# A fixed order on two engines for the main loop of two squared-ReLU MLPs

## The chip, the core and the metric

The kernel runs on one core of a Trainium2 chip. The metric is the device time of one execution in microseconds (us). Three runs of the kernel before took 2671.49 to 2674.87 us, median 2673.55 us.

The core's engines are named as in the profile: PE is TensorE (matmuls; PEld is its loading of weights), DVE is VectorE, ACT is ScalarE, POOL is GpSimd, SP is SyncE, which issues the DMAs. Each engine works through its own stream of instructions in order, and waits on semaphores for what others must finish first. Matmuls write to PSUM, which has 8 banks of 512 float32 a partition; here they are `bank[:, 0]` to `bank[:, 7]`.

## The reference

A trunk of two layers on x of 1024 positions by 1024 channels. Layer 0 mixes positions by gated linear attention and sparse attention, layer 1 by a spatial gating unit (SGU), and each is followed by an MLP:

```
def _squared_relu_mlp(x, w1, w2):          # w1: 1024 x 4096, w2: 4096 x 1024
    h = jax.nn.relu(x @ w1)
    return (h * h) @ w2
```

Each sub-layer f is applied as h = h + RMSNorm_post(f(RMSNorm_pre(h))). The change touches the MLPs alone.

## The kernel before

*Numbers in two halves.* Every float32 operand of a matmul is kept as a high and a low half: `split` (L149) makes the high half by a ScalarE copy (`acopy`, L137) and the low half by a VectorE subtraction (`sub`, L140). A product takes three matmuls of 512 columns: high x high, high x low, low x high (`PASS`, L36).

*Up-projection.* The 4096 hidden channels are cut into 32 chunks of 128. `fetch1` (L364) loads the columns of w1 for a chunk into a ring of two buffers (`raw`, 512 KB each) and multiplies them by the norm's gain on POOL (`gain`, L289). `put1` (L372) makes the halves in a ring of two (`w1r`; `ffa_w` in the profile). `f1(c, half)` (L350) computes one chunk for 512 positions: 24 matmuls into bank 0 or 1, then ReLU (L360) and square (L361) on ScalarE. Four such blocks belong to a pair of chunks: A11, A12 for positions 0 to 511 and A21, A22 for the rest.

*Down-projection.* For a pair of chunks it is a 2 x 2 product of blocks, (A11 A12; A21 A22) with (B11 B12; B21 B22) of w2, and is done with 7 products in place of 8. That takes 8 sums of blocks of 128 x 512: four of w2's blocks (`w_sums`, `w_prep`; the buffer `raw2` holds B, T1 is one more block) and four of the hidden blocks (`h_prep`). All 8 run on POOL (`minus` at L324, and the addition at L426). The seven operand pairs are split into `HS[0..6]` and `WS[0..6]` (`ffa_hTa`, `ffb_hTb` and `ffb_w` in the profile).

*Units.* `product(hh, i)` (L437) is one unit: the product i of 7 for one half hh of the 512 rows, 2 x 3 matmuls into a pair of banks, and two additions of the pair into `acc_of` (`ffb_acc`, L147). A pair of chunks has 14 units. `chain` gives bank pair, whether a new accumulation begins, and the target. The products that share a pair accumulate onto each other in PSUM, and each is read out in between. The pairs are banks 2/3, 6/7 and 4/5, the same for both halves.

*The loop.* It runs over 14 pairs p (`NS`) in each layer. An iteration emits the 14 units and, spread behind them, the 96 matmuls of the up-projection of the next pair (`ahead`, L451), then the preparation of its operands. The first iteration does 24 matmuls of the up-projection ahead of its first unit. The last four chunks are done plainly behind the loop (`out_proj`).

*What sets the order.* The kernel is written against a scheduler that keeps the data dependences and otherwise orders each engine's stream by its own model of when things will be ready. So the order in which the Python code emits units and preparation is a wish, and the streams differ from it.

Of the kernel before, what the change touches and what calls it, by code (L numbers as in the profile page):

```python
# [117 lines left out]
def tile_trunk(ctx, tc, x, norm_g, ffn_w1, ffn_w2, e_w_in, e_w_out, gla_w_gate, gla_b_gate,  # L118
# [27 lines left out]
    def add(o, a, b):  # L146
        dve.tensor_tensor(o, a, b, op=OP.add)  # L147
# [6 lines left out]
    def mm(o, lhsT, rhs, start, stop):  # L154
        pe.matmul(o, lhsT, rhs, start=start, stop=stop, skip_group_check=True)  # L155
# [167 lines left out]
    def minus(o, a, b):  # L323
        pool.tensor_tensor(o.f, a.f, b.f, op=OP.subtract)  # L324
# [4 lines left out]
    def ffn(l, hsrc, hdst, gi, nxt):  # L329
# [71 lines left out]
        def w_sums():  # L401
            minus(T1, B12, B11)
            minus(B12, B22, B12)

        def w_prep(i):

            split2((B11, B21, B11, T1, B12, B22, B21)[i], WS[i])
            if i == 0:
                minus(B11, B22, T1)
            if i == 1:  # L410
                minus(B21, B21, B11)

        def blocks(q):
            return [hf.get((2 * q + i, half)) for half in range(2) for i in range(2)]

        def h_prep(q, i):
            A11, A12, A21, A22 = blocks(q)
            if i == 0:
                split2(A11, HS[0])
                minus(A11, A11, A21)  # L420
            elif i == 1:
                split2(A12, HS[1])
                split2(A11, HS[4])
            elif i == 2:
                minus(A11, A22, A11)
                pool.tensor_tensor(A21.f, A21.f, A22.f, op=OP.add)  # L426
                split2(A11, HS[2])
                split2(A21, HS[3])
                minus(A12, A12, A11)
                split2(A12, HS[5])  # L430
                split2(A22, HS[6])


        chain = ((2, True, 0, 0), (6, True, 0, 0), (2, False, 0, 1), (4, True, 1, 1),
                 (2, False, 1, 1), (4, False, 0, 1), (2, False, 1, 0))

        def product(hh, i, first):  # L437
            b0, begin, ro, co = chain[i]
            for j in range(2):
                o = (2 * hh + j) * P  # L440
                for n, (a, b) in enumerate(PASS):
                    mm(bank[:, b0 + j, :], HS[i].r[:, a, o:o + P], WS[i].r[:, b],
                       begin and n == 0, n == 2)
            for j in range(2):
                o = acc_of[2 * hh + j + 4 * ro].f[:, co * 512:co * 512 + 512]
                if first and i in (0, 2, 3, 6):
                    acopy(o, bank[:, b0 + j, :])
                else:
                    add(o, o, bank[:, b0 + j, :])

        def ahead(q):  # L451
            a, b = 2 * q, 2 * q + 1
            yield from f1(a, 0)
            yield from f1(a, 1)
            put1(a + 2)
            yield from f1(b, 0)
            yield from f1(b, 1)
            put1(b + 2)

        fetch2(0)  # L460
        w_sums()
        for c in (0, 1):
            all_of(f1(c, 1))
            put1(c + 2)
            for i in ((0, 1, 2), (3, 4, 5, 6))[c]:
                w_prep(i)
        for i in (0, 1):
            h_prep(0, i)
        for p in range(NS):
            q, last = p + 1, p == NS - 1  # L470
            h_prep(p, 2)
            fetch2(q)
            for c in (2 * q + 2, 2 * q + 3):
                fetch1(c)
            if not last:
                w_sums()
            f = ahead(q)
            todo = 0
            while p == 0 and todo < 24:
                next(f)  # L480
                todo += 1
            for u in range(14):
                product(u // 7, u % 7, p == 0)
                n = 96 * (u + 1) // 14
                while todo < n:
                    next(f)
                    todo += 1
# [980 lines left out]
```

## Time and profile before

| | |
|---|---|
| median of three runs | 2673.55 us |
| the profiled execution | 2673.74 us |
| its span | 2671.9 us |
| PE busy | 2587.2 us, 97% |
| PE weight loads (PEld) | 2150.1 us, 80% |
| DVE busy | 1796.8 us, 67% |
| ACT busy | 1140.3 us, 43% |
| POOL busy | 743.5 us, 28% |
| mean granted clock of TensorE | 0.99 |

A busy TensorE is one that has a matmul in its pipeline, at whatever clock. So its busy share says little about how many matmuls a stretch holds; the count does. The first product of the loop of layer 0 starts 714.8 us into the span, that of layer 1 at 1989.5 us; each MLP with its loop takes about 640 us. [...]

### The profile page before, as it was taken

What the parts mean: (1) busy time and instruction counts of PE and PEld (TensorE: products, weight loads), DVE (VectorE), ACT (ScalarE), POOL (GpSimd) and SP (SyncE); (2) the same over time, 40 slices, a digit from 0 to 9 for tenths busy, and PEclk for the clock granted to TensorE, in tenths of its full rate; (3) what the DMA queues carried; (4) which work ended last, traced back from release to release, by engine and by line L of the source; (5) the groups of instructions that cost most, each with busy time, mean ns of one, the idle gap of its engine ahead of it and who ended that gap; (6) DMA issues with size and microseconds to landing.
All of it is one profiled execution on the core that took longest, in us unless ns stands there. A gap on an engine that the chain in (4) does not pass through costs nothing. (4 is left out here: it accounts for less than half of the span.)

```text
span 2671.9 us, 32503 instructions
## 1 busy us (share of the span) xinstructions
PE 2587.2 (97%) x12466; PEld 2150.1 (80%) x12466; DVE 1796.8 (67%) x2927; ACT 1140.3 (43%) x2127; POOL 743.5 (28%) x492
## 2 busy tenths in 40 slices
PE   8999999999999999999999999999999999999997
PEld 7888888888788887777877888888888888777786
DVE  5676578996757667776774248656675766777677
ACT  5556388885543333332354222242254333333233
POOL 2322133324433332333220011100142433333323
PEclk9999999999999999999999999999999999999999
DMA  4122211004311111111142101121241121111114
GB/s 131 52 61 75 60 44 37 17 13 153 139 48 54 49 48 48 48 53 35 63 140 81 47 24 48 40 95 40 78 135 42 46 63 45 51 48 48 40 40 142
DMA packets 150052, 168.31 MB, mean 63 GB/s; under 512 B 6549, under 2 KB 118409, under 8 KB 149897
## 3 DMA queue, kind: packets, MB, share of 16 engines
q1 hardware_dynamic: 149896, 166.24, 19.5%
q8 instruction: 98, 1.61, 0.2%
q14 instruction: 58, 0.47, 0.1%
HBM read 143.14 MB, written 23.07 MB: 62 GB/s over the span
## 5 line engine op out<-in xcount | busy, mean ns | idle before, releaser
L155 PE MATMUL bank<-base_x,ffa_w 128*128 128x512 f32 x3888 | 962.3, 392 | 2.7 <-DVE ffa_w L141 2.0
L155 PEld LDWEIGHTS bank<-base_x,ffa_w 128*128 128x128 f32 x3888 | 730.4, 189 | 159.1 <-ACT base_bnd L360 3.3
L147 DVE TENSOR_TENSOR ffb_acc<-ffb_acc,bank 128x512 f32<-128x512 f32 x784 | 520.6, 683 | 290.8 <-PE bank L155 282.1
L155 PE MATMUL bank<-ffb_w,ffb_hTb 128*128 128x512 f32 x1476 | 399.7, 395 | 17.5 <-DVE ffb_acc L147 15.3
L291 POOL TENSOR_TENSOR ffa_raw<-ffa_raw,base_cf 128x1024 f32<-128x1024 f32 x80 | 160.5, 2008 | 743.3 <-DMA ffa_raw<-in_ffn_w_dram 449.4
L155 PEld LDWEIGHTS bank<-ffb_w,ffb_hTb 128*128 128x128 f32 x1476 | 275.5, 189 | 90.7 <-DVE ffb_acc L147 29.0
L155 PE MATMUL bank<-ffb_w,ffa_hTa 128*128 128x512 f32 x1140 | 312.5, 398 | 25.1 <-DVE ffb_acc L147 21.7
L155 PEld LDWEIGHTS bank<-ffb_w,ffa_hTa 128*128 128x128 f32 x1140 | 216.5, 191 | 77.8 <-ACT ffa_hTa L138 12.2
L324 POOL TENSOR_TENSOR base_bnd<-base_bnd 128x512 f32<-128x512 f32 x84 | 125.9, 1499 | 299.7 <-DVE ffa_hTa L141 236.1
L155 PE MATMUL bank<-base_x,mv_w 128*128 128x512 f32 x768 | 185.8, 393 | 0.9 <-DVE nsq_qq L1166 0.9
L138 ACT ACTIVATE ffb_w<-ffb_raw 128x512 fp32r<-128x512 f32 x182 | 111.9, 622 | 171.4 <-PE bank L155 140.5
L141 DVE TENSOR_TENSOR ffb_w<-ffb_raw,ffb_w 128x512 fp32r<-128x512 f32 x182 | 159.7, 882 | 23.5 <-ACT ffb_w L138 23.4
L138 ACT ACTIVATE ffa_w<-ffa_raw 128x1024 fp32r<-128x1024 f32 x81 | 85.9, 1060 | 196.9 <-PE bank L155 185.0
L155 PEld LDWEIGHTS bank<-base_x,mv_w 128*128 128x128 f32 x768 | 140.7, 188 | 28.4 <-DVE nsq_qq L1166 1.1
L141 DVE TENSOR_TENSOR base_x<-bank,base_x 128x512 fp32r<-128x512 f32 x204 | 135.9, 683 | 30.7 <-ACT base_x L138 29.5
L141 DVE TENSOR_TENSOR ffa_w<-ffa_raw,ffa_w 128x1024 fp32r<-128x1024 f32 x81 | 105.0, 1297 | 64.6 <-ACT ffa_w L138 64.5
L138 ACT ACTIVATE base_x<-bank 128x512 fp32r<-128x512 f32 x204 | 117.6, 598 | 45.3 <-PE bank L237 27.1
L360 ACT ACTIVATE base_bnd<-bank 128x512 f32<-128x512 f32 x128 | 75.5, 590 | 128.5 <-PE bank L155 77.5
L138 ACT ACTIVATE ffb_hTb<-base_bnd 128x512 fp32r<-128x512 f32 x118 | 73.3, 627 | 121.1 <-PE bank L155 56.2
L141 DVE TENSOR_TENSOR ffb_hTb<-base_bnd,ffb_hTb 128x512 fp32r<-128x512 f32 x118 | 109.1, 929 | 20.6 <-ACT ffb_hTb L138 20.2
L138 ACT ACTIVATE ffa_hTa<-base_bnd 128x512 fp32r<-128x512 f32 (+1 forms) x93 | 59.7, 642 | 147.2 <-PE bank L155 83.6
L155 PE MATMUL bank<-nsa_kk,nsq_qq 128*128 128x512 f32 (+3 forms) x384 | 93.2, 353 | 4.1 <-ACT base_bnd L1285 2.1
(352 smaller groups left out, 3876.0 us busy)
## 6 DMA issues: line engine op xcount, KB each, us to landing
ffa_raw<-in_ffn_w_dram SPq DMA_DIRECT2D x64, 512.0 KB, 4.1
ffb_raw<-in_ffn_w_dram SPq DMA_DIRECT2D x30, 1024.0 KB, 4.8
hbuf<-base_bnd SPq DMA_DIRECT2D x24, 512.0 KB, 3.9
base_bnd<-hbuf SPq DMA_DIRECT2D x24, 512.0 KB, 3.5
ffa_raw<-in_o_w_in_dram SPq DMA_DIRECT2D x32, 256.0 KB, 2.9
ffa_raw<-in_o_w_in_dram SPq DMA_DIRECT2D x16, 512.0 KB, 4.0
gla_raw<-in_e_w_in_dram SPq DMA_DIRECT2D x30, 256.0 KB, 2.8
base_bnd<-in_x_dram SPq DMA_DIRECT2D x14, 512.0 KB, 3.4
```

Of the source, the lines that this page charges most:

```text
L138: act.activation(o, i, AF.Copy, **kw)
L141: dve.tensor_tensor(o, a, b, op=OP.subtract)
L147: dve.tensor_tensor(o, a, b, op=OP.add)
L155: pe.matmul(o, lhsT, rhs, start=start, stop=stop, skip_group_check=True)
L291: pool.tensor_tensor(raw, raw, gcol(gi)[:, k0:k0 + nk].unsqueeze(2).to_broadcast([P, nk, n]), op=OP.mult)
L324: pool.tensor_tensor(o.f, a.f, b.f, op=OP.subtract)
L360: act.activation(r.f, pb, AF.Relu)
```

## The change

Five things change in `ffn` and its helpers.

1. `keep` pins an instruction behind everything that was emitted before it on its engine (an edge of order, no wait). While `fixed[0]` is true, in the loop over the 14 units, every matmul, VectorE addition and VectorE subtraction is pinned. ScalarE, POOL and SyncE are not.
2. The 8 sums of an iteration move from POOL to VectorE (`minus` calls `sub`; A21 + A22 uses `add`).
3. The gain of w1 moves from one POOL operation of 128 x 1024 to eight ScalarE copies of 128 x 128 with a scale by partition.
4. A table of work by unit replaces the loose preparation. `before(p, u)` gives what is prepared with unit u: its sums and ScalarE copies are emitted ahead of the unit's matmuls, its VectorE subtractions behind the unit's two additions. `behind(p, u)` gives loads and sums behind the unit.
5. In the second half of the rows the bank pairs 2/3 and 6/7 are exchanged.

Over the kernel, VectorE gets 224 instructions more, ScalarE 512 more and POOL 288 fewer. The matmuls are the same in number and size.

```
+    def keep(ins):
+        if fixed[0]:
+            tc.keep_in_program_order(ins)
...
-        dve.tensor_tensor(o, a, b, op=OP.subtract)
+        keep(dve.tensor_tensor(o, a, b, op=OP.subtract))
...
-        pe.matmul(o, lhsT, rhs, start=start, stop=stop, skip_group_check=True)
+        keep(pe.matmul(o, lhsT, rhs, start=start, stop=stop, skip_group_check=True))
...
     def minus(o, a, b):
-        pool.tensor_tensor(o.f, a.f, b.f, op=OP.subtract)
+        sub(o.f, a.f, b.f)
...
-                gain(rw, gi, 0, KC, P)
+                for k in range(KC):
+                    acopy(rw[:, k], rw[:, k], scale=gcol(gi)[:, k:k + 1])
...
+        chain = ((0, True, 0, 0), (1, True, 0, 0), (0, False, 0, 1), (2, True, 1, 1),
+                 (0, False, 1, 1), (2, False, 0, 1), (0, False, 1, 0))
+        def unit(u, p):
+            hh, i = u // 7, u % 7
+            which, begin, ro, co = chain[i]
+            b0 = ((2, 6) if hh == 0 else (6, 2))[which] if which < 2 else 4
...
+        def before(p, u):
+            q, last = p + 1, p == NS - 1
+            work = []
+            if u < 4:
+                A11, A12, A21, A22 = blocks(p)
+                work += (([sums((sub, A11, A22, A11)), halves(A11, HS[2])]
+                          + ([] if p == 0 else [halves(B21, WS[6])])),
+                         [sums((add, A21, A21, A22)), halves(A21, HS[3])],
+                         [sums((sub, A12, A12, A11)), halves(A12, HS[5])],
+                         [halves(A22, HS[6])])[u]
+            if u == 4:
+                work += [halves1(2 * q + 1)]
+            if u == 7:
+                work += [halves1(2 * q + 2)]
...
+            elif u >= 8:
+                work += [halves((B11, B21, B11, T1, B12, B22)[u - 8], WS[u - 8])]
...
+        def behind(p, u):
+            q = p + 1
+            if u == 0:
+                fetch1(2 * q + 2)
+            if u == 1:
+                fetch2(q)
+            if u == 4:
+                fetch1(2 * q + 3)
...
+            if u == 5:
+                minus(T1, B12, B11)
...
+            fixed[0] = True
             for u in range(14):
-                product(u // 7, u % 7, p == 0)
...
+                work = before(p, u)
+                for w in work:
+                    next(w)
+                unit(u, p)
+                for w in work:
+                    all_of(w)
+                behind(p, u)
+                while done < 96 * (u + 1) // 14:
                     next(f)
-                    todo += 1
...
+                    done += 1
+            all_of(f)
+            fixed[0] = False
```

In the streams below, `ffa_w` with `base_x` are matmuls of the up-projection, `ffb_w` with `ffa_hTa` or `ffb_hTb` those of the units. A number behind a name is that of a buffer: `ffb_w_6217` to `ffb_w_6223` are WS[0] to WS[6] before, `ffb_w_6236` to `ffb_w_6242` after.

TensorE before, in an iteration past the middle of layer 0's loop, behind 8 matmuls of the up-projection and 3 of a unit:

```order
L155 MATMUL bank<-ffb_w_6219,ffa_hTa_6145 128x512 x3
L155 MATMUL bank<-ffb_w_6218,ffa_hTa_6144 128x512 x3
L155 MATMUL bank<-ffb_w_6219,ffa_hTa_6145 128x512 x3
L155 MATMUL bank<-ffb_w_6221,ffb_hTb_6224 128x512 x3
L155 MATMUL bank<-ffb_w_6218,ffa_hTa_6144 128x512 x3
L155 MATMUL bank<-ffb_w_6221,ffb_hTb_6224 128x512 x3
L155 MATMUL bank<-ffb_w_6223,ffb_hTb_6226 128x512 x6
L155 MATMUL bank<-ffb_w_6217,ffa_hTa_6144 128x512 x3
L155 MATMUL bank<-ffb_w_6220,ffa_hTa_6145 128x512 x4
L155 MATMUL bank<-ffb_w_6217,ffa_hTa_6144 128x512 x3
L155 MATMUL bank<-ffb_w_6220,ffa_hTa_6145 128x512 x2
L155 MATMUL bank<-base_x_72,ffa_w_6142 128x512 x20
```

Here 36 product matmuls, 39 with the 3 ahead of the first row, follow each other, of several units by threes, until the next 20 of the up-projection. TensorE after, from the first unit of an iteration:

```order
L162 MATMUL bank<-ffb_w_6236,ffa_hTa_6144 128x512 x6
L162 MATMUL bank<-base_x_71,ffa_w_6141 128x512 x6
L162 MATMUL bank<-ffb_w_6237,ffa_hTa_6144 128x512 x6
L162 MATMUL bank<-base_x_71,ffa_w_6141 128x512 x7
L162 MATMUL bank<-ffb_w_6238,ffa_hTa_6145 128x512 x6
L162 MATMUL bank<-base_x_71,ffa_w_6141 128x512 x7
L162 MATMUL bank<-ffb_w_6239,ffa_hTa_6145 128x512 x6
L162 MATMUL bank<-base_x_71,ffa_w_6141 128x512 x4
L162 MATMUL bank<-base_x_72,ffa_w_6141 128x512 x3
L162 MATMUL bank<-ffb_w_6240,ffb_hTb_6243 128x512 x6
```

Every unit stands as six, and 6 or 7 matmuls of the up-projection stand behind each; all iterations but the first have this order.

VectorE before, at the same place of the program as TensorE's rows:

```order
L147 TENSOR_TENSOR ffb_acc_6230<-ffb_acc_6230,bank 128x512
L147 TENSOR_TENSOR ffb_acc_6229<-ffb_acc_6229,bank 128x512
L147 TENSOR_TENSOR ffb_acc_6233<-ffb_acc_6233,bank 128x512
L147 TENSOR_TENSOR ffb_acc_6230<-ffb_acc_6230,bank 128x512
L147 TENSOR_TENSOR ffb_acc_6234<-ffb_acc_6234,bank 128x512
L141 TENSOR_TENSOR ffb_hTb_6224<-base_bnd,ffb_hTb_6224 128x512
L141 TENSOR_TENSOR ffb_w_6221<-ffb_raw_6216,ffb_w_6221 128x512
L147 TENSOR_TENSOR ffb_acc_6233<-ffb_acc_6233,bank 128x512
L141 TENSOR_TENSOR ffb_w_6219<-ffb_raw_6216,ffb_w_6219 128x512
L147 TENSOR_TENSOR ffb_acc_6234<-ffb_acc_6234,bank 128x512
L141 TENSOR_TENSOR ffb_hTb_6226<-base_bnd,ffb_hTb_6226 128x512
L141 TENSOR_TENSOR ffa_hTa_6145<-base_bnd,ffa_hTa_6145 128x512
```

The additions into `ffb_acc` stand in no order of units, with subtractions of halves between them. VectorE after, from the start of an iteration (the row `base_bnd<-base_bnd` with L148 is A22 - A11 or A12 - A11, that with L154 is A21 + A22):

```order
L148 TENSOR_TENSOR base_bnd<-base_bnd 128x512
L154 TENSOR_TENSOR ffb_acc_6246<-ffb_acc_6246,bank 128x512
L154 TENSOR_TENSOR ffb_acc_6247<-ffb_acc_6247,bank 128x512
L148 TENSOR_TENSOR ffa_hTa_6145<-base_bnd,ffa_hTa_6145 128x512
L148 TENSOR_TENSOR ffb_w_6242<-ffb_raw_6235,ffb_w_6242 128x512
L154 TENSOR_TENSOR base_bnd<-base_bnd 128x512
L154 TENSOR_TENSOR ffb_acc_6246<-ffb_acc_6246,bank 128x512
L154 TENSOR_TENSOR ffb_acc_6247<-ffb_acc_6247,bank 128x512
L148 TENSOR_TENSOR ffa_hTa_6145<-base_bnd,ffa_hTa_6145 128x512
L148 TENSOR_TENSOR base_bnd<-base_bnd 128x512
L154 TENSOR_TENSOR ffb_acc_6246<-ffb_acc_6246,bank 128x512
L154 TENSOR_TENSOR ffb_acc_6247<-ffb_acc_6247,bank 128x512
```

The sum for a later unit stands ahead of the two additions of a unit, and the subtraction of halves behind them.

ScalarE before, from a wide copy of w1 on in one iteration:

```order
L138 ACTIVATE ffa_w_6142<-ffa_raw 128x1024
L360 ACTIVATE base_bnd<-bank 128x512
L361 ACTIVATE base_bnd<-base_bnd 128x512
L138 ACTIVATE ffb_hTb_6224<-base_bnd 128x512
L138 ACTIVATE ffb_w_6221<-ffb_raw_6216 128x512
L138 ACTIVATE ffa_hTa_6145<-base_bnd 128x512
L138 ACTIVATE ffb_hTb_6226<-base_bnd 128x512
```

The ReLU and the square of a block stand behind the wide copy. ScalarE after, at the start of an iteration:

```order
L138 ACTIVATE ffa_w_6142<-ffa_raw 128x1024
L367 ACTIVATE base_bnd<-bank 128x512
L368 ACTIVATE base_bnd<-base_bnd 128x512
L138 ACTIVATE ffb_hTb_6245<-base_bnd 128x512
L138 ACTIVATE ffa_hTa_6145<-base_bnd 128x512 x2
L138 ACTIVATE ffb_hTb_6244<-base_bnd 128x512
L367 ACTIVATE base_bnd<-bank 128x512
```

Here it is the copy for the next iteration's second chunk that stands ahead of the ReLU and the square of A22, and the copies for HS[6], HS[2], HS[3] and HS[5] follow.

## Rows read from the trace of the kernel before

**Rows 1.** Share of the span and instructions of each engine, from the page.
```profile
PE 2587.2 (97%) x12466; PEld 2150.1 (80%) x12466; DVE 1796.8 (67%) x2927; ACT 1140.3 (43%) x2127; POOL 743.5 (28%) x492
```

**Rows 2.** By stretches: matmuls (x) behind PE, then PEld, DVE, ACT, POOL, granted clock.
```profile
715.00:1355.00 640.00, 617.52 (x2653) 499.44 (x2652) 439.80 (x614) 227.04 (x373) 208.39 (x136) 0.99 0.17 53
755.00:955.00 200.00, 200.00 (x884) 165.68 (x883) 132.73 (x186) 71.83 (x116) 71.44 (x45) 1.00 0.16 51
1035.00:1235.00 200.00, 182.92 (x755) 144.81 (x755) 146.80 (x197) 64.36 (x106) 72.96 (x47) 0.96 0.15 45
1989.50:2629.50 640.00, 619.84 (x2670) 502.09 (x2669) 442.98 (x613) 225.83 (x371) 208.45 (x136) 0.99 0.16 51
2029.50:2229.50 200.00, 200.00 (x884) 165.40 (x882) 136.64 (x187) 72.09 (x116) 71.97 (x46) 1.00 0.16 51
2309.50:2509.50 200.00, 185.30 (x771) 146.71 (x770) 148.59 (x200) 65.61 (x108) 72.97 (x47) 0.97 0.16 51
```

**Rows 3.** The same view at one hole, and right behind it.
```profile
1041.00:1046.00 5.00, 1.81 (x8) 1.21 (x7) 5.00 (x6) 1.89 (x3) 5.00 (x4) 0.96 0.00 0
1045.50:1052.50 7.00, 6.30 (x16) 4.36 (x16) 7.00 (x10) 2.25 (x5) 2.73 (x2) 0.51 0.19 48
```

**Rows 4.** TensorE's waits in layer 0's MLP: total us, times, longest us.
```profile
PE bank L155 <- DVE ffb_acc L147: 18.5, 20, 3.2
```

**Rows 5.** Timeline at that hole: start, us, engine, line, operation, idle before it.
```profile
...
1032.25 2.88 PE L155 MATMUL bank<-ffb_w,ffa_hTa 128*128 128x512 f32 x12
...
1037.27 3.07 DVE L147 TENSOR_TENSOR ffb_acc<-ffb_acc,bank 128x512 f32<-128x512 f32 x5
...
1039.69 1.89 POOL L291 TENSOR_TENSOR ffa_raw<-ffa_raw,base_cf 128x1024 f32<-128x1024 f32 x1
1040.26 1.88 DVE L141 TENSOR_TENSOR ffb_hTb<-base_bnd,ffb_hTb 128x512 fp32r<-128x512 f32 x1
...
1040.40 0.96 PE L155 MATMUL bank<-ffb_w,ffb_hTb 128*128 128x512 f32 x3 [0.24 <-DVE ffb_acc L147]
...
1041.55 1.71 POOL L426 TENSOR_TENSOR base_bnd<-base_bnd 128x512 f32<-128x512 f32 x1
1042.06 1.74 DVE L141 TENSOR_TENSOR ffb_w<-ffb_raw,ffb_w 128x512 fp32r<-128x512 f32 x1
...
1043.29 0.63 ACT L138 ACTIVATE ffa_hTa<-base_bnd 128x512 fp32r<-128x512 f32 x1 [1.50 <-POOL base_bnd L426]
1043.72 0.68 DVE L147 TENSOR_TENSOR ffb_acc<-ffb_acc,bank 128x512 f32<-128x512 f32 x1
...
1044.55 2.81 PE L155 MATMUL bank<-ffb_w,ffa_hTa 128*128 128x512 f32 x8 [3.19 <-DVE ffb_acc L147]
```

**Rows 6.** By tile: count, then shortest, median and longest in ns.
```profile
L141 DVE TENSOR_TENSOR ffb_w<-ffb_raw,ffb_w x182: 675/686/2406, 708.2 to 2622.7; 128x512 fp32r<-128x512 f32 x182
L324 POOL TENSOR_TENSOR ffb_raw<-ffb_raw x56: 1282/1297/2157, 708.9 to 2583.6; 128x512 f32<-128x512 f32 x56
...
L141 DVE TENSOR_TENSOR ffa_w<-ffa_raw,ffa_w x81: 1206/1226/2352, 642.1 to 2559.7; 128x1024 fp32r<-128x1024 f32 x81
```

**Rows 7.** ScalarE by form: count, busy us, mean ns, idle before.
```profile
L138 ACT ACTIVATE ffb_w<-ffb_raw 128x512 fp32r<-128x512 f32 x182 | 111.9, 622 | 171.4 <-PE bank L155 140.5 <-POOL ffb_raw L324 14.2 <-DVE ffb_acc L147 12.3
...
L138 ACT ACTIVATE ffa_w<-ffa_raw,base_cf 128x512 fp32r<-128x512 f32 x14 | 9.8, 722 | 5.2 <-PE bank L155 3.4 <-DMA ffa_raw<-in_o_w_in_dram 1.5
...
L193 ACT ACTIVATE base_cf<-base_cf 128x1 f32<-128x1 f32 x48 | 9.4, 198 | 9.9 <-DVE base_cf L204 8.0 <-DVE base_cf L267 1.7
```

**Rows 8.** Timeline of ScalarE at the end of a projection.
```profile
882.32 1.06 ACT L138 ACTIVATE ffa_w<-ffa_raw 128x1024 fp32r<-128x1024 f32 x1 [1.12 <-PE bank L155]
883.29 0.58 ACT L360 ACTIVATE base_bnd<-bank 128x512 f32<-128x512 f32 x1
883.90 0.64 ACT L361 ACTIVATE base_bnd<-base_bnd 128x512 f32<-128x512 f32 x1
```

**Rows 9.** Loads of w2: from issue to landing.
```profile
DMA to landing us min/median/max: 3.0/4.8/6.8
```

More of the change, by code (lines that the diff above doesn't have):

```diff
@@ L399, in ffn, with halves, sums @@
         B11, B12, B21, B22 = (raw2[:, i, j] for i in range(2) for j in range(2))
[L401 to L411, printed above, removed]
-        def blocks(q):
[L414 to L438, printed above, removed]
+        def blocks(q):
+            return [hf[2 * q + i, half] for half in range(2) for i in range(2)]
+        def halves(src, slot):
+            acopy(slot.r[:, 0], src.f)
+            yield
+            sub(slot.r[:, 1], src.f, slot.f[:, 0])
+        def sums(*ops):
+            for op, o, a, b in ops:
+                op(o.f, a.f, b.f)
+            yield
+        chain = ((0, True, 0, 0), (1, True, 0, 0), (0, False, 0, 1), (2, True, 1, 1),
[4 more added lines that the diff above has]
+            b0 = ((2, 6) if hh == 0 else (6, 2))[which] if which < 2 else 4
             for j in range(2):
@@ L451, in ahead @@
         def ahead(q):
[L452 to L458, printed above, removed]
-        fetch2(0)
[L461 to L468, printed above, removed]
-        for p in range(NS):
[L470 to L479, printed above, removed]
+            for c in (2 * q, 2 * q + 1):
+                for half in range(2):
+                    yield from f1(c, half)
@@ new lines, in before @@
+        def before(p, u):
[12 more added lines that the diff above has]
+                work += [halves1(2 * q + 2)]
+            if u >= 8 and last:
+                if u < 12:
+                    work += [halves((B11, B12, B21, B22)[u - 8], WS[u - 8])]
+            elif u >= 8:
+                work += [halves((B11, B21, B11, T1, B12, B22)[u - 8], WS[u - 8])]
+                if u >= 10:
+                    A11, A12, A21 = (hf.get((2 * q + i, half)) for i, half in
+                                     ((0, 0), (1, 0), (0, 1)))
+                    work += ([halves(A11, HS[0])], [], [halves(A12, HS[1])],
+                             [halves(A11, HS[4])])[u - 10]
+            return work
@@ new lines, in ffn @@
+        fetch2(0)
+        all_of(f1(0, 1))
+        all_of(halves1(2))
+        fetch1(3)
+        all_of(f1(1, 1))
+        minus(T1, B12, B11)
+        minus(B12, B22, B12)
+        split2(B11, WS[0])
+        minus(B11, B22, T1)
+        split2(hf[0, 0], HS[0])
+        minus(hf[0, 0], hf[0, 0], hf[0, 1])
+        split2(B21, WS[1])
+        minus(B21, B21, B11)
+        split2(hf[1, 0], HS[1])
+        for i, b in ((2, B11), (3, T1), (4, B12)):
+            split2(b, WS[i])
+        split2(hf[0, 0], HS[4])
@@ L480, in ffn @@
+        for i, b in ((5, B22), (6, B21)):
+            split2(b, WS[i])
+        for p in range(NS):
+            f, done = ahead(p + 1), 0
+            while p == 0 and done < 24:
                 next(f)
[L481 removed]
+                done += 1
+            fixed[0] = True
             for u in range(14):
[L483 to L487 removed]
```

37 lines of the change are left out of this document (22 added, 15 removed).

## The prediction

> **What bounds the kernel now.** I read the shares of the engines first [rows 1]: TensorE is busy for 97% of the span and VectorE for 67%, so only time in which TensorE issues below its full rate can be won. The second view is the table by stretches, taken over the two MLPs [rows 2]. What to see there is the count of matmuls, not the busy time, since TensorE is also "busy" while it runs at half clock. A quiet stretch of 200 us in either MLP holds 884 matmuls of 512 columns, one every 0.2262 us. In 640 us that would be 2829. The MLP of layer 0 has 2653 and that of layer 1 has 2670, so 176 and 159 matmuls are missing, or 39.8 and 36.0 us: 75.8 us in all. They are not spread evenly. One stretch of 200 us in each loop (755 and 771 matmuls) lacks 129 and 113 of them, and its granted clock is 0.96 and 0.97, which by itself is 8 and 6 us. The rest, some 62 us, is waiting.
>
> The third view is the list of waits, which puts TensorE's waiting down to VectorE's additions into `ffb_acc`: 18.5 us in 20 waits, and the same again in the second loop [rows 4]. The fourth is the timeline of one such place [rows 5], and it says why the additions are late. The scheduler has put 12 product matmuls side by side and has no up-projection left to go between the next ones. Then the operands are missing. POOL does a gain of 1.89 us ahead of the sum that the next operand needs, and while POOL works two subtractions on VectorE take 1.88 and 1.74 us. The addition that would free the bank stands behind both, so TensorE stops for 3.19 us. At 1041 to 1046 us TensorE is busy for 1.81 of 5 us, and right behind that it gets 0.51 of its clock for about 7 us [rows 3]. [...] So a hole is paid for twice.
>
> **The change, part by part.**
>
> *Order on TensorE and VectorE.* An iteration is 14 units of 6 product matmuls plus 96 of the up-projection: 180 matmuls, 180 x 0.2262 = 40.7 us, 2.9 us a unit. After, 6 or 7 up-projection matmuls stand behind every unit, so between two uses of one bank pair lie another unit and two such groups: 6 + 7 + 7 matmuls, 4.5 us, in which the two additions must be done. Two additions take 1.3 us when nothing stands ahead of them. Exchanging banks 2/3 and 6/7 in the second half keeps that true where one half of the chain meets the other; with the old numbers the second half would begin on the pair that the first had just finished, with 7 matmuls (1.6 us) between.
>
> *Load on VectorE.* Per iteration: 28 additions, 14 subtractions of halves and now 8 sums, 50 instructions of 128x512, and two of 128x1024. VectorE has no such sum in the trace of before. The nearest row is the subtraction for `ffb_w`: median 0.686 us, longest 2.406 [rows 6]. The long ones are those that meet POOL: in the timeline 1.88, 1.74, and the POOL ops beside them 1.71 to 1.89 [rows 5]. After, POOL has nothing to do in the loops, so I take the median. Lower bound: five additions in a row take 3.07 us, which is 0.60 apart. So 50 x 0.60 to 0.69 and 2 x 1.23 [rows 6] is 32.5 to 37.0 us of 40.7. It fits, and VectorE's growth lies beside TensorE's work; if it did not fit, the whole loop would run at VectorE's pace (a rival below).
>
> *Load on ScalarE.* The gain goes from one POOL op to eight ScalarE ops of 128 columns, 16 an iteration. Such an op is not in the trace. Bounds: 0.198 us for one column and 0.722 us for 512 columns with a scale by column [rows 7]; a straight line between gives 0.33, so 5.3 us an iteration (3.2 to 11.6). With 14 halves at 0.62 [rows 7], two wide copies at 1.06 and four pairs of ReLU and square at 0.58 + 0.64 [rows 8], ScalarE has 21 us of 40.7, at worst 27. It hides behind TensorE. [...]
>
> *The start of an iteration* is the tightest place. VectorE's first instruction there is A22 - A11, and A22 is the last up-projection of the iteration before. On ScalarE the wide copy for `ffa_w` stands ahead of its ReLU and square; the three take 2.22 us from start to end [rows 8]. Queued on VectorE behind that subtraction are both additions of unit 0 and the lower half of the operand of unit 2: 2.2 + 0.7 + 1.3 + 0.7 = 4.9 us after the end of that projection. TensorE needs this half after unit 0, 6 matmuls, unit 1, 7 matmuls and the first two of unit 2, 27 x 0.2262 = 6.1 us, less 0.2 us for the pipeline of the last matmul. Unit 3 follows 2.9 us later, with about 3.1 us of VectorE work before it. So there is 0.8 to 1.0 us to spare, and I cost it at nothing.
>
> *A new wait.* T1 = B12 - B11 stands behind the additions of unit 5 on VectorE, and waits for the 1 MB of w2; behind it stand the additions of unit 6. The buffer comes free when unit 0's halves are done (5.5 us into the iteration), landing takes 3.0 to 6.8 us [rows 9], so the data is there at 12.3 us at the latest, and the subtraction's turn comes at 17.5. Nothing is lost. The DMAs keep their number and sizes.
>
> *What stays or is added.* Ahead of the loop five sums come to VectorE, and the first up-projection of chunk 2 is now pinned ahead of unit 0; it needs the chunk's halves, a ScalarE copy of 1.06 and a subtraction of 1.23 us, of which the last 14 matmuls of the chunk before it cover 3.2 us, if VectorE is free. Units 0 to 3 of the first iteration follow each other without up-projection between. I bound this by 0 and 5 us a layer and take 2.5, so 5 us. Outside the MLPs the order is as before.
>
> **Sum.** The profiled execution took 2673.7 us, its span 2671.9 us; the median of the runs is 2673.55, so it stands for them. 2673.7 - 75.8 + 5 = **2603 us**, a gain of 2.6%.
>
> **Rivals.**
>
> *A short stall in every iteration* (chance 0.13). If the start of an iteration is 1 us later than I count (0.8 to 1.0 to spare), every one of the 28 loses about 1 us at units 2 and 3: 2603 + 28 = 2631. For it: VectorE's fixed order lets nothing pass a late A22. Against: the later units have 2 us and more, so a delay does not add up.
>
> *The clock falls by itself* (0.06). If short waits remain, and the granted clock of the worst stretches (0.96) [rows 2] becomes that of both loops, 28 x 40.7 x 0.04 = 46 us come back: 2649. Against: the quiet stretches use the same three bank pairs at 1.00, and the low clock in rows 3 follows a hole. [...]
>
> *Given back outside* (0.08). The gain comes, but the prologues, or the ScalarE gains inside the stages before, cost 25 us a layer more than the 2.5 I take: about 2650. Nothing in the profile asks for it.
>
> *VectorE becomes the bound, and the kernel slower* (0.04). Place: the 24 SBUF subtractions and sums of an iteration. If the long ones were not POOL's doing, an op would cost c, and an iteration 28 x 0.60 + 22c + 2 x 1.8c = 16.8 + 25.6c us. It passes 40.7 us at c = 0.93, eats the whole gain (2.5 us in each of 28) at c = 1.03, and at c = 1.16, a usual long one in the timeline, it is 46.5 us: 28 x 5.8 = 162 us, 2765. Against: the median is 0.686.
>
> *It does nothing* (0.02): the holes move to other places of the same size, 2673.
>
> **How the numbers follow.** The forecast has 0.67, with 2594 to 2614 as its own range (0 to 5 us a layer of added cost, and a few matmuls that I may have put down to the loops wrongly). The range that holds 8 in 10 takes in the first rival and reaches toward the next two: 2594 to 2640. About 0.2%, 5 us, is what a measurement of this kernel can tell from no change. Faster: 0.67 + 0.13 + 0.06 + 0.08 = 0.94; same 0.02; slower 0.04.
>
> **What would show it.** Right: in the MLPs the stretches hold 177 matmuls per 40 us throughout and the granted clock is 1.00 there; VectorE's 128x512 subtractions have a mean near 0.69 us in place of 0.88; POOL is nearly empty in the loops; TensorE's waits for `ffb_acc` are gone. Wrong: VectorE busy without a gap while TensorE waits for it, a wait in every iteration at units 2 and 3, or a clock below 1.00 with no hole ahead of it.

## The result and the profile after

The changed kernel takes 2597.4 us (median of four runs, 2595.65 to 2597.74) against 2672.87 us before: ratio 0.9716, interval 0.9699 to 0.9733. It is 75.5 us faster; the forecast was 2603, 70 us faster.

The profiled execution took 2597.74 us. Its shares of the span, from the page:

```profile
PE 2555.6 (98%) x12466; PEld 2148.0 (83%) x12466; DVE 1856.6 (72%) x3151; ACT 1301.7 (50%) x2639; POOL 295.2 (11%) x204
```

The table by stretches, with the columns of [rows 2]; the first three rows have the windows of layer 0's rows there, the last is layer 1's loop:

```profile
715.00:1355.00 640.00, 640.00 (x2837) 530.04 (x2836) 505.68 (x802) 323.27 (x647) 12.94 (x6) 1.00 0.19 62
755.00:955.00 200.00, 200.00 (x884) 165.62 (x883) 167.02 (x254) 98.77 (x200) 0.00 (x0) 1.00 0.17 53
1035.00:1235.00 200.00, 200.00 (x884) 165.59 (x883) 167.93 (x256) 94.90 (x190) 0.00 (x0) 1.00 0.17 53
1960.00:2570.00 610.00, 610.00 (x2692) 504.99 (x2691) 480.07 (x740) 292.89 (x586) 8.76 (x4) 1.00 0.17 55
```

TensorE is never idle here, its clock is 1.00, and the stretch that held 755 matmuls holds 884. In the same 640 us there are 2837 matmuls in place of 2653. TensorE's waits over the whole span (total us, times, longest):

```profile
PE bank L184 <- DMA base_bnd<-in_gla_norm_dram: 4.8, 1, 4.8
PE bank L244 <- DVE base_bnd L261: 4.3, 1, 4.3
PE bank L162 <- ACT base_bnd L1330: 3.0, 5, 1.9
PE bank L244 <- DVE in_y L238: 2.2, 1, 2.2
PE bank L162 <- DVE ffa_w L148: 2.1, 1, 2.1
```

The additions into `ffb_acc`, which led this list before [rows 4], do not appear. By tile (count, shortest/median/longest ns, as in [rows 6]), VectorE's subtraction for `ffb_w` and the new gain pieces on ScalarE:

```profile
L138 ACT ACTIVATE ffa_raw<-ffa_raw,base_cf x512: 384/387/407, 638.9 to 2501.7; 128x128 f32<-128x128 f32 x171
...
L148 DVE TENSOR_TENSOR ffb_w<-ffb_raw,ffb_w x182: 683/686/693, 709.3 to 2521.4; 128x512 fp32r<-128x512 f32 x182
```

The subtraction's longest is 693 ns, where before it was 2406. A timeline of ScalarE (start, us, then the row) has one gain:

```profile
867.48 2.46 ACT L138 ACTIVATE ffa_raw<-ffa_raw,base_cf 128x128 f32<-128x128 f32 x8 [2.70 <-DMA ffa_raw<-in_ffn_w_dram]
```

Eight pieces take 2.46 us. Each is 0.39 long by itself, but they overlap: their starts are 0.29 apart (0.31 for the first two).

The start of an iteration in the timeline, on TensorE, then ScalarE and VectorE. Unit 0 starts at 880.27, unit 1 at 882.99, unit 2 at 885.94:

```profile
880.27 1.52 PE L162 MATMUL bank<-ffb_w,ffa_hTa 128*128 128x512 f32 x6
881.63 1.52 PE L162 MATMUL bank<-base_x,ffa_w 128*128 128x512 f32 x6
882.99 1.52 PE L162 MATMUL bank<-ffb_w,ffa_hTa 128*128 128x512 f32 x6
884.35 1.75 PE L162 MATMUL bank<-base_x,ffa_w 128*128 128x512 f32 x7
885.94 1.52 PE L162 MATMUL bank<-ffb_w,ffa_hTa 128*128 128x512 f32 x6
...
880.24 1.06 ACT L138 ACTIVATE ffa_w<-ffa_raw 128x1024 fp32r<-128x1024 f32 x1 [0.73 <-PE bank L162]
...
882.48 0.69 DVE L148 TENSOR_TENSOR base_bnd<-base_bnd 128x512 f32<-128x512 f32 x1 [1.71 <-ACT base_bnd L368]
883.09 1.28 DVE L154 TENSOR_TENSOR ffb_acc<-ffb_acc,bank 128x512 f32<-128x512 f32 x2
884.29 0.68 DVE L148 TENSOR_TENSOR ffa_hTa<-base_bnd,ffa_hTa 128x512 fp32r<-128x512 f32 x1
```

The wide copy waits for the end of A22's projection and starts at 880.24. The half (the row `ffa_hTa<-base_bnd,ffa_hTa`) that unit 2 needs is done at 884.97, and the third matmul of unit 2 wants it at 885.94 + 2 x 0.2262 = 886.39. So 1.4 us are to spare.

### The profile page after: what moved, and what is told of

Its sections match the earlier page's. It is cut to its first block, busy times and chain, and to the rows that moved or that the text cites. A ratio compares the mean times of both kernels' runs of the same rounds, so it can differ in the third digit from the quotient of the medians.

```text
span 2596.0 us, 33054 instructions
## 1 busy us (share of the span) xinstructions
PE 2555.6 (98%) x12466; PEld 2148.0 (83%) x12466; DVE 1856.6 (72%) x3151; ACT 1301.7 (50%) x2639; POOL 295.2 (11%) x204
## 4 chain that ended last, share of the span: by engine, by line
PE 87%; DVE 5%; ACT 3%; issue 2%; DMA 1%; POOL 1%; SPq 0%; DVEq 0%; POOLq 0%; ACTq 0%
PE bank L162 85%; PE bank L1346 1%; DVE base_x L148 1%; PE bank L244 1%; DVE base_cf L1329 1%; DVE mv_P L1339 1%; ACT base_x L138 1%; POOL mv_P L260 0%; ACT base_bnd L1330 0%; DMA base_bnd<-in_e_w_out_dram 0%; DMA base_bnd<-in_x_dram 0%; DVE sgu_v L683 0%; ACT mv_P L1330 0%; ACT base_bnd L210 0%; DMA base_bnd<-rbuf 0%
## 5 line engine op out<-in xcount | busy, mean ns | idle before, releaser
L154 DVE TENSOR_TENSOR ffb_acc<-ffb_acc,bank 128x512 f32<-128x512 f32 x784 | 524.5, 685 | 137.9 <-PE bank L162 134.7
L162 PE MATMUL bank<-ffb_w,ffb_hTb 128*128 128x512 f32 x1476 | 374.8, 389 | 0.0
L138 ACT ACTIVATE ffa_raw<-ffa_raw,base_cf 128x128 f32<-128x128 f32 x512 | 156.9, 389 | 267.6 <-DMA ffa_raw<-in_ffn_w_dram 267.6
L162 PE MATMUL bank<-ffb_w,ffa_hTa 128*128 128x512 f32 x1140 | 288.1, 389 | 0.0
L260 POOL TENSOR_TENSOR ffb_acc<-ffb_acc,base_bnd 128x1024 f32<-128x1024 f32 x15 | 36.0, 2400 | 1287.8 <-ACT base_bnd L210 1283.9
L148 DVE TENSOR_TENSOR base_x<-bank,base_x 128x512 fp32r<-128x512 f32 x204 | 136.0, 683 | 33.5 <-ACT base_x L138 32.4
L148 DVE TENSOR_TENSOR ffb_w<-ffb_raw,ffb_w 128x512 fp32r<-128x512 f32 x182 | 124.6, 686 | 8.5 <-ACT ffb_w L138 4.4
L148 DVE TENSOR_TENSOR ffa_w<-ffa_raw,ffa_w 128x1024 fp32r<-128x1024 f32 x81 | 99.8, 1234 | 41.7 <-ACT ffa_w L138 41.5
L1329 DVE TENSOR_REDUCE base_cf<-bank 128x1 f32<-128x640 f32 (+7 forms) x128 | 88.5, 698 | 12.1 <-PE bank L162 11.5
L162 PE MATMUL bank<-base_x,nsa_V 128*128 128x512 f32 x264 | 94.4, 431 | 2.6 <-DVE base_x L148 1.3
```

Of the source, the lines that this page charges most:

```text
L138: act.activation(o, i, AF.Copy, **kw)
L148: keep(dve.tensor_tensor(o, a, b, op=OP.subtract))
L154: keep(dve.tensor_tensor(o, a, b, op=OP.add))
L162: keep(pe.matmul(o, lhsT, rhs, start=start, stop=stop, skip_group_check=True))
L260: pool.tensor_tensor(acc, acc, gpost.f, op=OP.mult)
L1329: dve.reduce_max(out=nm, in_=sc[:, 0:W], axis=AX, negate=True)
```

## The experiments

| kernel | order | banks | sums and gain | us | ratio to before, interval |
|---|---|---|---|---|---|
| before | scheduler | old | POOL | 2672.9 | |
| changed | pinned | exchanged | moved | 2597.4 | 0.9716 (0.9699 to 0.9733) |
| order_only | pinned | exchanged | POOL | 2613.1 | 0.9770 (0.9755 to 0.9784) |
| moves_only | scheduler | old | moved | 2669.9 | 0.9983 (0.9973 to 0.9992) |
| old_banks | pinned | old | moved | 2602.4 | 0.9728 (0.9714 to 0.9743) |
| free | scheduler | exchanged | moved | 2597.5 | 0.9713 (0.9699 to 0.9728) |
| banks_only | scheduler | exchanged | POOL | 2599.5 | 0.9726 (0.9712 to 0.9741) |
| moves_banks | scheduler | exchanged | moved | 2597.4 | 0.9720 (0.9705 to 0.9734) |
| free_old_banks | scheduler | old | moved | 2669.2 | 0.9984 (0.9974 to 0.9994) |
| one_pin | one matmul pinned | old | POOL | 2642.4 | 0.9886 (0.9869 to 0.9902) |
| pool_sums | pinned | exchanged | only sums on POOL | 2608.6 | 0.9768 (0.9752 to 0.9785) |
| pool_gain | pinned | exchanged | only gain on POOL | 2600.9 | 0.9735 (0.9720 to 0.9749) |
| dve_14 | as changed, 14 subtractions more | | | 2727.9 | 1.0208 (1.0193 to 1.0223) |
| dve_7 | as changed, 7 subtractions more | | | 2599.9 | 0.9729 (0.9715 to 0.9744) |

My theory was the prediction's: the fixed order earns the time, with POOL emptied so that VectorE's additions are not late; the banks are a side condition.

### Parts of the change alone

**order_only**: the changed kernel with sums and gain given back to POOL.

```
-        sub(o.f, a.f, b.f)
+        pool.tensor_tensor(o.f, a.f, b.f, op=OP.subtract)
...
-                for k in range(KC):
-                    acopy(rw[:, k], rw[:, k], scale=gcol(gi)[:, k:k + 1])
+                gain(rw, gi, 0, KC, P)
```

> The changed kernel with its fixed order, but the 8 sums of an iteration and the gain of w1 back on POOL as before. Theory A (order): the holes came from an order that ran out of up-projection matmuls between units, so the fixed order alone removes them. VectorE's subtractions stay long beside POOL (mean near 0.88 us), 28 x 0.60 + 14 x 0.88 + 2 x 1.3 = 31.7 us of 40.7, which fits; the sum A22 - A11 takes 1.3 to 1.7 us on POOL where VectorE took 0.7, which uses up most of the 0.8 to 1.0 us to spare: 2597 to 2612 us. Theory B (contention): the holes came from subtractions that POOL makes long, and in an order that lets nothing pass they cost at least 1 us in each of 28 iterations: 2630 us or more.

2613.1 us, 1 us above the range of theory A and far below theory B. It keeps most of the gain, and past the first iterations its loops have no wait of TensorE. Nearly all that it lacks lies ahead of the loops and in their first iterations: from each MLP's first up-projection matmul to the end of the loop's first iteration TensorE loses 12.4 us more than in the changed kernel, of the 13.5 us by which the two profiled executions differ.

**moves_only**: the kernel before with sums and gain moved, the scheduler's order and the old banks.

```
-        pool.tensor_tensor(o.f, a.f, b.f, op=OP.subtract)
+        sub(o.f, a.f, b.f)
...
-                pool.tensor_tensor(A21.f, A21.f, A22.f, op=OP.add)
+                add(A21.f, A21.f, A22.f)
...
-                gain(rw, gi, 0, KC, P)
+                for k in range(KC):
+                    acopy(rw[:, k], rw[:, k], scale=gcol(gi)[:, k:k + 1])
```

> The kernel before in its free order, with only the sums moved to VectorE and the gain to ScalarE. Theory A (order): the scheduler still bunches units, holes and half clock stay for the most part, 2640 to 2680 us. Theory B (contention): without POOL beside it VectorE keeps up, and most of the 75 us is gone, 2600 to 2620 us.

2669.9 us: the move earns 0.17%. A stretch of its trace, then its first wait over the whole span and that of the kernel before:

```profile
1035.00:1235.00 200.00, 188.88 (x806) 150.66 (x805) 153.58 (x239) 88.77 (x184) 0.00 (x0) 0.99 0.15 46
```

```profile
PE bank L155 <- DVE ffb_acc L147: 33.8, 45, 1.9
...
PE bank L155 <- DVE ffb_acc L147: 37.0, 40, 3.2
```

POOL does nothing in this stretch, and still 78 of 884 matmuls are missing and TensorE waits for the additions. POOL was not what made the holes. The longest wait is shorter (1.9 us against 3.2), there are more of them, and the total is nearly the same.

**old_banks**: the changed kernel without the exchange.

```
-            b0 = ((2, 6) if hh == 0 else (6, 2))[which] if which < 2 else 4
+            b0 = (2, 6, 4)[which]
```

> The changed kernel without the exchange of bank pairs in the second half: units 6 and 7, and 13 and the next 0, use banks 2/3 with 7 up-projection matmuls (1.6 us) between. If the exchange matters: the additions need 0.2 + 0.7 us for the first bank and 0.6 more for the second, so VectorE may be at most 0.7 us behind; where it is more, 0.3 to 0.5 us at each of 56 seams, 2612 to 2625 us, with waits for ffb_acc at units 7 and 0. If it does not: 2597 us, within 3.

2602.4 us, between the two cases expected. Under the pinned order the exchange is worth 5 us, all of it in the first iteration of each layer, where TensorE waits for 1.9 and 2.0 us for ScalarE's copies of `ffb_acc` and in the changed kernel does not. Past that, the 7 matmuls at the seam cover the additions even when the pair is the same.

**free**: the changed kernel with nothing pinned.

```
-            fixed[0] = True
+            fixed[0] = False
```

> The changed kernel with nothing pinned: the same code, moves and banks, but the scheduler orders TensorE and VectorE freely. Theory A (order): holes come back, 2630 to 2670 us. Theory B (contention), or the emission alone being enough: 2597 to 2610 us.

2597.5 us, the same as with the pins. So the pinned order is not needed, and my theory falls: what is left are the banks and the table.

### The banks

**banks_only**: the kernel before, with this alone:

```
             b0, begin, ro, co = chain[i]
+            if hh == 1 and b0 != 4:
+                b0 = 8 - b0
```

> The kernel before with one edit: banks 2/3 and 6/7 exchanged in the second half of the units. No pin, no moves, old table. Theory C (banks): with the old banks a unit at each seam stands on a pair that is still being read, the scheduler pulls up-projection matmuls ahead to fill that place, and some iterations later there are none left; in the built stream of this kernel no run of more than 24 product matmuls is left, where before has runs of 39. So most of the 75 us goes: 2597 to 2615 us. Theory A (the pinned order is needed): 2640 us or more.

2599.5 us: one edit earns 73 of the 75.5 us. Stretches, and the `ffb_w` subtraction (count, busy us, mean ns, idle before):

```profile
1035.00:1235.00 200.00, 200.00 (x884) 165.61 (x883) 157.62 (x215) 73.24 (x117) 80.71 (x50) 1.00 0.17 53
```

```profile
L141 DVE TENSOR_TENSOR ffb_w<-ffb_raw,ffb_w 128x512 fp32r<-128x512 f32 x182 | 147.9, 816 | 19.1 <-ACT ffb_w L138 17.4
```

POOL works for 80.7 of 200 us and the subtractions are still stretched to a mean of 816 ns (882 before, 686 after), and no matmul is missing. The slow subtractions stand at the holes of before, but by themselves they make none.

**moves_banks** adds the same three lines to moves_only.

> The run moves_only (sums on VectorE, gain on ScalarE, free order: 2669.88 us) with the banks exchanged as well. Theory C (banks): as the changed kernel, 2595 to 2603 us. Theory A (the table of work by unit, or the pin, is needed): still above 2640 us.

2597.4 us, level with the changed kernel, without table or pins.

**free_old_banks**: the changed kernel without pins and without the exchange, so free's and old_banks's edits together.

> The changed kernel with nothing pinned and without the exchange of banks: table of work, sums on VectorE, gain on ScalarE. Theory C (banks): runs of 39 and 30 product matmuls are in its built stream again, so holes come back, 2655 to 2675 us, as moves_only. Theory D (the new table of work by unit is what keeps the up-projection spread): 2597 to 2610 us.

2669.2 us, the holes are back. So in the scheduler's order the exchange decides, whatever else is done. Why is seen in TensorE's streams of layer 0. I counted in them how many up-projection matmuls are issued by the end of an iteration, less 96 for each iteration before that one (89 is the order as emitted), and the longest run of product matmuls without one between:

| kernel | ahead at the end of iterations 1, 2, 3, 4, 5, 6 | then | longest runs in iterations 6 to 14 |
|---|---|---|---|
| before | 106, 140, 168, 199, 234, 240 | 240 | 12 to 48, from iteration 7 on 21 or more |
| moves_only, free_old_banks | 113, 151, 185, 226, 240, 240 | 240 | 18 to 45 |
| banks_only | 92, 89, 89, 89, 89, 89 | 89 | 12 |
| moves_banks, free | 89, 93, 93, 93, 93, 93 | 93 | 18 |
| changed, old_banks | 89, 89, 89, 89, 89, 89 | 89 | 6 |

With the old numbers the units 6 and 7, and 13 and 0 of the next iteration, use one pair in a row. The scheduler then spends some 30 to 40 more up-projection matmuls in each iteration, until it is 240 ahead, where all three kernels stop. From there the product matmuls stand alone, and the holes begin. That is why the first 200 us of each loop were whole and the later ones not [rows 2]. That the scheduler spends them to fill the seam is inferred from the edit that ends it, and the streams bear it out in part: in iterations 2 to 4 the kernel before has 12 to 18 up-projection matmuls at a seam where the order as emitted has 7, which is about half of the growth of the lead; the rest stands at the other uses of pair 2/3 and within units. The exchange also does a second thing: it gives pair 2/3 five of the 14 units in place of eight. No run has the one without the other, so which of the two makes the scheduler spend its lead stays open.

**one_pin** is to take only the lead away: the kernel before, with the first up-projection matmul of an iteration pinned.

```
+                    pin[0] = q > 1 and c == a and half == 0
                     yield from f1(c, half)
```

(`mm` pins the next matmul when `pin[0]` is set, and clears it.)

> The kernel before, with one edit: of the 96 matmuls of the up-projection of an iteration, the first is pinned behind what is emitted ahead of it on TensorE (behind unit 0), from the second iteration on: 13 pinned matmuls a layer. Banks, POOL's work and everything else are as before. In TensorE's stream before, the up-projection runs ahead of the units by 28 to 44 matmuls more in each of the first iterations of a layer, until it is 240 ahead; from there runs of 21 to 48 product matmuls stand without up-projection between. With the pin it stays at 137 ahead, and no run is longer than 18. Theory C (the old banks cost only because this lead is used up): 2597 to 2606. Rival (the old banks cost by themselves, by TensorE's waiting at the seam where pair 2/3 is used twice in a row, so that only their exchange or a full order helps): 2650 to 2674. Rival (the exchange of banks helps since it keeps additions and POOL's work apart): 2630 to 2674.

2642.4 us: theory C, that the old banks cost only by the lead, misses by 36 us, and the first rival by 8. The second rival's range holds it, but the rival itself had fallen by other runs: free_old_banks has the holes with POOL empty, banks_only has none with POOL busy. The lead stays at 137 and the long runs are gone (15 at most from the third iteration on), which earns 30 of the 73 us. TensorE's timeline at the end of one iteration, then its first wait over the span, then two stretches:

```profile
893.16 1.52 PE L157 MATMUL bank<-ffb_w,ffb_hTb 128*128 128x512 f32 x6
896.21 1.66 PE L157 MATMUL bank<-ffb_w,ffa_hTa 128*128 128x512 f32 x6 [1.52 <-DVE ffb_acc L147]
897.71 5.38 PE L157 MATMUL bank<-base_x,ffa_w 128*128 128x512 f32 x23
```

```profile
PE bank L157 <- DVE ffb_acc L147: 33.1, 22, 1.8
```

```profile
715.00:1315.00 600.00, 583.69 (x2558) 478.81 (x2557) 442.75 (x599) 221.17 (x357) 216.22 (x136) 1.00 0.17 54
...
875.00:915.00 40.00, 38.48 (x170) 31.52 (x169) 30.39 (x41) 13.24 (x22) 15.81 (x10) 1.00 0.17 53
```

The last unit of an iteration (WS[6]) and the first of the next (WS[0]), both on banks 2/3, follow each other with nothing between. My pin holds the first block of 24 up-projection matmuls of an iteration behind unit 0, and the third block, which uses the same bank, comes behind the first. The second and the fourth block are not held: the scheduler runs these 48 ahead (89 + 48 = 137) and has used them up before the seam. TensorE waits 1.5 us there, 22 times for 33 us, and the clock is 1.00 over the 600 us of layer 0's loop. That is 33 of the 43 us that one_pin lacks against banks_only. With 7 matmuls at the same seam (1.6 us of work) old_banks has no such wait. So the old banks cost in two ways: the scheduler spends its lead, and where no matmul is left for the seam, the seam itself costs 1.5 us. As one_pin still has part of the lead, it does not tell the two apart fully; a pin ahead of unit 0, on every block, was not run.

### What the moves are for under the pinned order

**pool_sums** and **pool_gain** are the two halves of order_only's diff.

> The changed kernel with only the 8 sums of an iteration given back to POOL; the gain stays on ScalarE. The kernel with both on POOL took 2613.1, 15.7 us more, all of it ahead of the loops and in their first iteration. If the sums make it (five sums of 1.3 us each one after the other on POOL ahead of the first units, against 0.69 on VectorE): 2608 to 2613. If the gain makes it (1.9 us on POOL ahead of the first chunks): 2597 to 2600. If it is VectorE's and POOL's working beside each other, both kernels lie between.

> The changed kernel with only the gain of w1 given back to POOL; the sums stay on VectorE. If the sums make the 15.7 us: 2597 to 2600. If the gain makes them: 2608 to 2613, with TensorE waiting ahead of the loops for the halves of the first chunks. In the loops no wait in either case.

2608.6 and 2600.9 us: of 15.7 us the sums on POOL make 11.2, as expected, and the gain 3.5, though the interval of pool_gain overlaps that of the changed kernel. TensorE, then POOL, then ScalarE, where layer 1's loop begins in pool_sums, and the stretch behind the stop:

```profile
1959.15 2.88 PE L162 MATMUL bank<-ffb_w,ffa_hTa 128*128 128x512 f32 x12
1964.65 3.51 PE L162 MATMUL bank<-ffb_w,ffb_hTb 128*128 128x512 f32 x8 [2.62 <-ACT ffb_acc L138]
...
1960.26 3.88 POOL L424 TENSOR_TENSOR base_bnd<-base_bnd 128x512 f32<-128x512 f32 x3
...
1959.63 2.45 ACT L138 ACTIVATE ffa_raw<-ffa_raw,base_cf 128x128 f32<-128x128 f32 x8 [3.36 <-DMA ffa_raw<-in_ffn_w_dram]
...
1964.02 0.58 ACT L138 ACTIVATE ffb_acc<-bank 128x512 f32<-128x512 f32 x1
```

```profile
1964.65:1968.16 3.51, 3.51 (x9) 2.83 (x10) 3.29 (x6) 2.61 (x5) 0.00 (x0) 0.56 0.00 0
```

Three sums in a row take POOL 3.88 us beside the first units. TensorE stops for 2.62 us in a fixed order that nothing can pass; it waits for ScalarE's copy that reads unit 0's bank, and that copy stands behind a gain, three copies of halves and a ReLU, with which ScalarE is busy from 1959.63 on. How the sums on POOL bring ScalarE into this order is not shown. The 8 matmuls behind the stop are 0.4 us apart, not 0.23, at a mean clock of 0.56. Here a hole in a pinned prologue is paid for twice, as the prediction said of the loops.

### How much room VectorE and the iteration's start have

**dve_14** does each of the 14 subtractions of halves twice, **dve_7** every other one.

```
-            sub(slot.r[:, 1], src.f, slot.f[:, 0])
+            for _ in range(2):
+                sub(slot.r[:, 1], src.f, slot.f[:, 0])
```

> The changed kernel with each of the 14 subtractions of halves of an iteration done twice (the second writes the same values again), 14 more VectorE instructions of 128x512 in every iteration, and 14 ahead of each loop. VectorE has 34.0 us of 40.7 busy in the quiet stretches of the changed kernel. If one more costs 0.60 us, an iteration needs 42.4 us and VectorE becomes the bound: 28 x 1.7 = 48 us, about 2645 us; at 0.69 us each 43.7 us, 28 x 3.0 = 84 us, about 2680 us. If VectorE has more room than its busy time says: 2600 us. Holes at half clock would come on top.

2727.9 us, slower than the kernel before and above both figures worked out ahead (2645 and 2680). The start of an iteration in its trace, TensorE, then VectorE, then TensorE at the start of the next iteration; then stretches:

```profile
902.25 0.70 PE L162 MATMUL bank<-ffb_w,ffa_hTa 128*128 128x512 f32 x2 [1.44 <-ACT ffa_hTa L138]
904.09 2.08 PE L162 MATMUL bank<-ffb_w,ffa_hTa 128*128 128x512 f32 x4 [1.13 <-DVE ffa_hTa L148]
...
899.30 1.41 DVE L148 TENSOR_TENSOR ffb_hTb<-base_bnd,ffb_hTb 128x512 fp32r<-128x512 f32 x2
900.82 0.69 DVE L148 TENSOR_TENSOR base_bnd<-base_bnd 128x512 f32<-128x512 f32 x1
901.43 1.28 DVE L154 TENSOR_TENSOR ffb_acc<-ffb_acc,bank 128x512 f32<-128x512 f32 x2
902.62 1.41 DVE L148 TENSOR_TENSOR ffa_hTa<-base_bnd,ffa_hTa 128x512 fp32r<-128x512 f32 x2
...
947.88 0.70 PE L162 MATMUL bank<-ffb_w,ffa_hTa 128*128 128x512 f32 x2 [1.42 <-ACT ffa_hTa L138]
949.71 1.20 PE L162 MATMUL bank<-ffb_w,ffa_hTa 128*128 128x512 f32 x4 [1.13 <-DVE ffa_hTa L148]
...
954.16 1.19 PE L162 MATMUL bank<-ffb_w,ffa_hTa 128*128 128x512 f32 x4 [1.12 <-DVE ffa_hTa L148]
```

```profile
902.00:909.60 7.60, 6.21 (x20) 4.54 (x21) 7.50 (x13) 1.28 (x3) 0.00 (x0) 0.78 0.38 139
947.60:955.20 7.60, 5.07 (x20) 3.45 (x21) 7.50 (x13) 1.28 (x3) 0.00 (x0) 1.00 0.40 138
755.00:955.00 200.00, 185.66 (x781) 147.92 (x780) 186.38 (x291) 84.20 (x171) 0.00 (x0) 0.97 0.15 47
```

The added work is 14 x 0.66 = 9.2 us an iteration (0.66 is the mean busy time of a VectorE instruction in the changed kernel, 167.02 us over 254), and VectorE had 40.7 - 34.0 = 6.7 to spare (167.02 of 200 us busy is 34.0 of 40.7). By load alone 2.5 us an iteration would be lost, but 130.5 / 28 = 4.7 are. They are lost at the start of the iteration. In the iteration at 902 TensorE stops twice at unit 2, for 2.6 us, and has a mean of 0.78 of its clock over 7.6 us, which is 1.7 us. The next one has the same two stops at a clock of 1.00, and a third at unit 3 instead, 3.7 us in all. The waits for `ffa_hTa` in layer 0's loop and for `ffb_hTb` in layer 1's sum to 79.8 us, 2.9 an iteration; the rest comes in the iterations where the clock falls (0.97 over 200 us, in the last row above), and in the matmuls around the stops.

> The changed kernel, with every other of the subtractions of halves of 128x512 done twice, so 7 more an iteration (the result is the same). 7 x 0.66 = 4.6 us on top of 34.0 us busy is 38.6 of 40.7 us an iteration. Theory A (VectorE's room is a threshold, and so is the 0.8 to 1.0 us to spare at the start of an iteration, of which at most one doubled subtraction takes 0.66): 2597 to 2606. Rival B (each subtraction more costs the same, half of what 14 cost: 130.5 us / 2): about 2662. Rival C (the start of an iteration is already used up, so 0.66 us is lost in each of 28 and the clock falls behind each wait): 2615 to 2650.

2599.9 us, 2.5 us above the changed kernel, as theory A had it: 4.6 us more an iteration still fit. As far as these two points show, the price of VectorE's work is a threshold between 4.6 and 9.2 us more an iteration, not a rate.

## Why the prediction was right, and where not

**The amount** was right, to within a few us. 75.8 us were to come back in the loops [rows 2], and 2673.7 - 75.8 = 2597.9 against 2597.7 in the profiled execution. That these agree to 0.2 us is luck in part. The MLPs from their first up-projection matmul to their last product matmul, two rows before and two after:

```profile
686.13:1389.13 703.00, 677.28 (x2933) 548.40 (x2931) 486.49 (x709) 263.87 (x442) 229.35 (x147) 0.99 0.18 59
1964.21:2659.49 695.28, 674.82 (x2922) 547.37 (x2921) 483.96 (x689) 250.08 (x418) 233.97 (x148) 0.99 0.18 57
...
684.57:1353.36 668.79, 664.53 (x2949) 550.15 (x2947) 527.00 (x845) 342.10 (x681) 19.17 (x8) 0.99 0.20 65
1924.71:2585.22 660.51, 660.21 (x2922) 546.01 (x2921) 514.12 (x804) 322.55 (x645) 19.24 (x9) 1.00 0.19 61
```

They are 69.0 us shorter and hold 16 matmuls more (3.6 us), so about 72.6 us came back there, and some 3 us outside the MLPs, which the forecast did not count. Counting missing matmuls against a quiet stretch measured the size of the gain before any cause was known. What the missing time is made of was read wrongly: the prediction has some 62 us of waiting, but in the same rows TensorE is idle for 640 - 617.52 and 640 - 619.84, 42.6 us together. The rest is time in which it counts as busy and has no full rate, at a low clock (0.51 right behind the hole of [rows 3]) or around a stop.

**The cause** was half right. The prediction named TensorE's order (product matmuls side by side with no up-projection left) [rows 5]: the streams and one_pin bear this out. It put the lateness of the additions down to POOL as well: moves_only has the holes with POOL empty, and banks_only has none with POOL busy. And it took the bank exchange for a detail that keeps the seam safe, while free, banks_only and free_old_banks show that without pins it decides. Pins and exchange are two ways to the same end: old_banks has only the pins, free only the exchange, and each has nearly the whole gain. What the profile before could have told: the holes begin when a lead of up-projection matmuls has run up to its limit, after six iterations, and that can be counted in the streams.

**The hole is paid for twice.** True of some holes only. The clock is 1.00 in both loops once the holes are gone, and it falls behind the stop in pool_sums (0.56 over 3.51 us) and behind some of those in dve_14 (0.78 over 7.6 us). But in one_pin 11 stops of 1.5 us in layer 0's loop leave it at 1.00 over 600 us, and in dve_14 the same two stops go with 0.78 in one iteration and with 1.00 in the next. What brings the clock down is not shown.

**Load on VectorE.** 34.0 us an iteration, within 32.5 to 37.0; the subtraction's mean is 686 ns. **Load on ScalarE.** 98.77 of 200 us is 20.1 of 40.7 us; 21 was worked out. The gain piece was put at 0.33: it is 0.39 long and 0.29 from the next. It stays hidden: TensorE is busy for all of the 200 us.

**The start of an iteration.** 0.8 to 1.0 us to spare were counted, 1.4 are there: the chain from the end of A22's projection takes 4.7 us in place of 4.9, and TensorE comes to it a little later than counted. That it is the tightest place was right: dve_14 stops there first.

**T1's wait** cost nothing: no wait of TensorE in the loops. **The prologue** was put at 5 us and is about nothing: the first 110 us of layer 0's MLP hold 474 matmuls before and 472 after, the first 100 us of layer 1's 448 and 450. This is the mis-sized term, and it is most of the 5.6 us between forecast and result. The wait that was feared there, for the wide subtraction of chunk 2, does not come: TensorE's one wait for `ffa_w` (2.1 us) lies 1566 us into the span, in the stage between the MLPs, and the kernel before has it too (2.0 us). With sums and gain on POOL (order_only) the kernel is 15.7 us slower.

**The rivals.** No stall in any iteration, no fall of the clock in the loops (1.00), nothing given back outside. The clock rival needed short waits that remain; none does, and with three pairs of banks in use in every iteration the granted clock of the loops is 1.00. VectorE as the bound is real, though not at the present load: with 4.6 us more an iteration (dve_7) nothing much happens, with 9.2 (dve_14) the kernel is slower than before by 2.1%.

## What to carry to other kernels

Where a scheduler orders the work, look at each place where two accumulations in a row use the same PSUM banks, and at how many of the accumulations one pair of banks carries: it may spend work from elsewhere to fill the gap, and the loss appears many iterations later, at another place. Count the matmuls of a stretch against a quiet one to get the size of a loss, but change one thing at a time to get its cause; here three lines of bank numbers were worth as much as a fixed order of two engines. A hand-made order needs its prologue as well covered as its loop, since nothing can pass a late operand.

## What was not expected of the hardware

- A stop of 1.5 us in nearly every iteration of some 42 us did not lower TensorE's clock (one_pin, 1.00 over 600 us). Two stops, of 1.44 and 1.13 us with two matmuls between, went with a mean clock of 0.78 in one iteration of dve_14, and two of 1.42 and 1.13 us with 1.00 in the next.
- VectorE's subtractions for `ffb_w` had a mean of 816 ns beside POOL (banks_only), against 686 without it (the changed kernel), and yet banks_only and moves_banks differ by 2.1 us, with intervals that overlap.
- ScalarE pieces of 128 columns overlap: 0.39 us each by their records, 0.29 apart.
